# One layer of sparse attention and a gated recurrence: splits of the recurrence at a slot's head, a group of products half a step later, key roots by quarters

## Chip, core and metric

The kernel runs on one core of a Trainium2 chip. A core has a matrix engine (PE, whose weight loads the profile lists as PEld), a vector engine (DVE), a scalar engine (ACT), a general engine (POOL) and a queue engine for transfers (SP). Each works through its own list of instructions in order, and waits at an instruction until what it depends on has been signalled. The metric is the device time of one execution in microseconds; lower is better.

## What is computed

One inference step of a hybrid decoder layer, for a prompt of 512 tokens and for 8 sample sequences of 8 tokens each, 576 columns in all, in fp32. The reference, cut to what matters here:

```python
def _project(x, norm_g, w_in, q_norm_g, k_norm_g):
    z = jnp.einsum('btd,dc->btc', _rms(x, norm_g), w_in)
    ...                                        # q, kv, gates, x_rnn, g_rnn, ... are columns of z
    kv_sel = jnp.stack([_rms(kv[:, :, 1, 0], k_norm_g[1]), kv[:, :, 1, 1]], axis=2)
    kv_win = jnp.stack([_rms(kv[:, :, 2, 0], k_norm_g[2]), kv[:, :, 2, 1]], axis=2)

def _sel_win_sample(q, kv_sel_new, kv_win_new, sel_idx, sel_valid, cache_sel, page_table, cache_win, q_pos):
    ...                                        # softmax over cached and new keys, compressed branch beside it

def _rglru(x_ext, h0, conv_w, conv_b, w_rg, b_rg, w_ig, b_ig, lru_lambda):
    xc = conv_b
    for k in range(CONV_W):
        xc = xc + x_ext[:, k:k + T] * conv_w[k]
    xb = xf.reshape(B, T, RNN_BLOCKS, RNN_BLOCK_DIM)
    r = jax.nn.sigmoid(jnp.einsum('btnd,nde->btne', xb, w_rg).reshape(B, T, D_RNN) + b_rg)
    i = jax.nn.sigmoid(jnp.einsum('btnd,nde->btne', xb, w_ig).reshape(B, T, D_RNN) + b_ig)
    log_a = -LRU_C * r * jax.nn.softplus(-lru_lambda)
    a, u = jnp.exp(log_a), jnp.sqrt(-jnp.expm1(2.0 * log_a)) * (i * xf)
    ...                                        # h = a * h + u over the tokens
```

The two branches are gated, projected to 2048 columns, merged, and go through one output projection.

## The kernel before

**Products in slots.** Every large product is made of three products of halves: an operand is split into a rounded high part and the rest, and high by high, low by high and high by low are summed in one bank of PSUM (lines 1798 to 1800). The columns go in two halves of 288. A slot is 24 such matmuls: one output tile, one half of the columns, 8 blocks of the sum. The weights are split two slots or so ahead of their use: ACT makes `whi` (line 233), DVE makes `wlo` (line 239).

**What sets the order.** Nothing is scheduled by a planner while the chip runs. The program is written out slot by slot, and each engine gets its instructions in the order of writing. In one slot come, one after the other: the weights' high part; what `at(slot, f)` has put at the slot's head (`later`); the step of the prompt's or the samples' attention that is due; the weights' low part; the evacuation of a finished tile (`evac`: for a gate of the recurrence, an ACT line 576 and a DVE line 577); what `at(slot, f, True)` has put behind (`behind`); and last the slot's 24 matmuls. So for ACT and DVE, `later` stands ahead of the attention's step and the evacuation, `behind` after them.

**Keys of the prompt.** For each of four groups of heads, `norms` works the keys' root mean squares into the keys: `small` (lines 622 to 634), `root` (a reciprocal on line 639 and a product on line 640), `split` (lines 646 to 653). These stand in slots among the prompt's attention: scores on PE, row maxima on DVE (line 742), exponentials on ACT (line 746), the sums' reciprocal on DVE (lines 750 and 751), the scaling of the probabilities on POOL (line 754), and their transposition on PE (line 761).

**Samples.** `sample_steps` lists the samples' attention by `put(step, half, order, f)`: four pairs of sequences, a step is two slots, `half` says which of them, and `order` sorts within the slot; orders of one slot go from small to large. `x_turn_` (lines 1000 and 1004, PE) turns the probabilities and values of the compressed branch, `x_turned` (lines 1011 to 1013, ACT) copies them to `vx`, `x_out` (line 1021, 48 small matmuls on PE) multiplies them. `x_sum` (line 969) is a small sum that stands later. `s_turned` (line 1083, ACT) copies the turned probabilities of cached keys out of the banks `t`.

**Recurrence.** Eight chunks of 128 channels, `rnn_chunk(c, xr)`, called about every 12th slot beside the samples' attention. Its parts stand in the slots behind the call: the convolution's taps (lines 1276 and 1277, DVE), `split` (line 1221 on ACT and 1222 on DVE for the block weights `bd`, lines 1291 on ACT and 1292 on DVE for the channels `xb`), the gates' matmuls (line 1302, PE, into a bank `s` and a bank `t`) with their tanh (line 1305, ACT), `decay` (lines 1308 to 1310, ACT) and `scan` (lines 1315 to 1323). PSUM has two banks `g`, `s` and `t` each, and one `o` and one `m`; a bank's next use waits until its last reader has signalled.

The order in time is: projection of the prompt's heads with the prompt's attention (to about 720 us), the samples' attention with the recurrence (720 to 1024 us), the remaining projections and the output products (1025 to 1644 us).

Of the kernel before, what the change touches and what calls it, by code (L numbers as in the profile page):

```python
# [32 lines left out]
HF = 288  # L33
# [80 lines left out]
def nsa_rglru_step(ctx, tc, a, o):  # L114
# [15 lines left out]
    def bank(tag):  # L130
        t = ps.tile([128, 512], F, tag=tag, name=tag, bufs=banks[tag])
        current[tag] = (current[tag] + [t])[-banks[tag]:]
        return t
# [15 lines left out]
    def C(name):  # L149
        at, n = CST[name]  # L150
        return cst[:, at:at + n]

    def P(name, i=0):
        return par[:, PAR[name][0] + i:PAR[name][0] + i + 1]
# [36 lines left out]
    for n, (kind, m, units) in enumerate(tiles):  # L191
# [19 lines left out]
        for u in range(len(units)):  # L211
            late = len(units) == 1 or u == 0 and tiles[n - 1][0][0] == "G"
            at = base - 2 if late else base - 3 if u == 0 else base - 1
# [109 lines left out]
    for c in range(8):  # L323
        for b in range(2):
            k = 2 * c + b
            x = xs[c][:, b]
# [41 lines left out]
    def at(slot, fn, last=False):  # L368

        (behind if last else later).setdefault(slot, []).append(fn)  # L370

    now = [0]
# [13 lines left out]
    def store(fn, delay=2):  # L386
        at(now[0] + delay, fn)
# [3 lines left out]
    def evac(kind, h, b):  # L391
# [165 lines left out]
        elif name == "rx":  # L557
# [9 lines left out]
            if h == 1:  # L567
                A.activation(xr[:, 515:603].rearrange("p (b s) -> p b s", s=11)[:, :, 3:11],
                             b[:, n0:HF].rearrange("p (t b) -> p b t", b=8), AF.Copy)
                rnn_chunk(c, xr)  # L570
# [33 lines left out]
    def norms(g):  # L604

        k, v, rq = held["k"], held["ksq"], held["rq"]
        cc, sq = held["cc"]
        m = bank("m")
        T.matmul(m[:, :16], C("bones"), sq, start=True, stop=True)
        V.tensor_scalar(sq, m[:, :16], 1.0 / HD, EPS, op0=OP.mult, op1=OP.add)  # L610
        A.activation(sq, sq, AF.Sqrt)
        A.activation(rq, rq, AF.Sqrt)
        A.activation(v, v, AF.Sqrt)
        m = bank("t")
        T.transpose(m[:16, :128], cc, ident)
        vc = VCB[g % 2]
        A.activation(vc[:16, 0, :], m[:16, 64:128], AF.Copy)
        V.tensor_sub(vc[:16, 1, :], m[:16, 64:128], vc[:16, 0, :].bitcast(F))
        VC[g] = vc

        def small():
            V.reciprocal(sq, sq)
            V.reciprocal(rq, rq)
            RQ[g] = rq
            kc2 = pp["p"].tile([128, 32], R, tag="kc2", name="kc2", bufs=2)
            kc = pp["p"].tile([128, 16], F, tag="kc", name="kc", bufs=2)
            lo = slice(0, 64)
            V.scalar_tensor_tensor(kc[lo], cc[lo], P("gk0")[lo], sq[lo], OP.mult, OP.mult)
            for hl in range(2):
                d = slice(hl * 64, hl * 64 + 64)  # L630
                A.activation(kc2[d, 0:16], kc[lo], AF.Copy)
            for hl in range(2):
                d = slice(hl * 64, hl * 64 + 64)
                V.tensor_sub(kc2[d, 16:32], kc[lo], kc2[lo, 0:16].bitcast(F))
            KC[g] = kc2

        def root(h):
            hs = slice(h * HF, h * HF + HF)
            V.reciprocal(v[:, hs], v[:, hs])
            V.scalar_tensor_tensor(k[:, hs], k[:, hs], P("gk12"), v[:, hs], OP.mult, OP.mult)  # L640
            if h == 1:
                store(lambda: S.dma_start(o["kv"][2 * KG + g], k))

        def split(br):
            me = slice(br * 64, br * 64 + 64)
            V.tensor_copy(kn[(g % 2) * 64:(g % 2) * 64 + 64, g // 2, br, :], k[me, 512:576])
            kh = pp["a"].tile([128, SEQ], R, tag="k", name="kh", bufs=4)
            kl = pp["a"].tile([128, SEQ], R, tag="k", name="kl", bufs=4)
            other = slice(64 - br * 64, 128 - br * 64)
            A.activation(kh[me], k[me, :SEQ], AF.Copy)  # L650
            A.activation(kh[other], k[me, :SEQ], AF.Copy)
            V.tensor_sub(kl[me], k[me, :SEQ], kh[me].bitcast(F))
            V.tensor_sub(kl[other], k[me, :SEQ], kh[me].bitcast(F))
            K[g, br] = (kh, kl)

        for n, f in enumerate((small, lambda: root(0), lambda: root(1), lambda: split(0), lambda: split(1), lambda: ready.add(g))):
            if n in FULL:
                full.add(now[0] + 1 + n)
            at(now[0] + 1 + n, f, n < 5)

    ready, full = set(), set()
# [13 lines left out]
    for g in range(KG):  # L675
        for i in range(4):
            for br in range(3):
                x = Group()
# [473 lines left out]
    def sample_steps():  # L1152

        steps = {}

        def put(t, half, order, f, *args):
            steps.setdefault(2 * t + half, []).append((order, len(steps.get(2 * t + half, [])), f, args))

        for x in pairs:
            s = 2 + 6 * x.n
            if x.b[0].b >= KEPT:
                for y in x.b:
                    put(s - 5, 1, 0, c_fetch, y)
            put(s - 2, 0, 9, q_pair, x)
            e = s - 3 if x.n else s - 2
            put(e, 0, 0, c_square, x)
            put(e, 1, 5, c_norm, x)
            put(e, 1, 7, c_root, x)  # L1170
            put(e + 1, 1, 7, c_keys, x)
            put(s, 0, 4, x_scores, x)
            put(s, 0, 8, x_exp, x)
            put(s, 1, 7, x_prob, x)
            put(s, 1, 9, x_new, x)
            put(s + 1, 1, 5, x_sum, x)
            put(s + 1, 1, 6, x_select, x)
            for k, n2 in enumerate((4, 0, 1, 2, 3)):
                t = s + 1 + k
                put(t - 1, 0, 0, k_load, x, n2)  # L1180
                put(t, 1, 0, v_load, x, n2)
                put(t, 0, 4, k_scores, x, n2)
                put(t, 0, 8, k_max, x, n2)
                put(t, 0, 9, s_exp, x, n2)
                put(t + 1, 0, 1, s_turn, x, n2)
                put(t + 1, 0, 1.5, s_turned, x, n2)
                put(t + 2, 0, 2, s_out, x, n2)
            put(s + 5, 1, 9, s_factors, x)
            put(s + 6, 1, 7, s_total, x)
            put(s + 6, 1, 1, x_turn_, x)  # L1190
            put(s + 6, 1, 1.5, x_turned, x)
            put(s + 7, 0, 4.5, x_out, x)
            put(s + 7, 1, 8, s_sum, x)
            put(s + 8, 1, 5, s_fin, x)
            put(s + 8, 1, 8, s_put, x)
        for t in range(max(steps) + 1):
            fs = [f for _, _, f, _ in steps.get(t, [])]
            taken.extend(f for f in fs if f in (x_scores, k_scores, s_turn, x_turn_, c_norm))
            for _, _, f, args in sorted(steps.get(t, []), key=lambda e: e[:2]):
                f(*args)  # L1200
            yield (t + 1) / (max(steps) + 1)
# [15 lines left out]
    def split_bd(c):  # L1217
        t = bd[c]
        hi = rp_["p"].tile([128, 2, 128], R, tag="bdh", name="bdh", bufs=1)
        lo = rp_["p"].tile([128, 2, 128], R, tag="bdl", name="bdl", bufs=1)  # L1220
        A.activation(hi, t, AF.Copy)
        V.tensor_sub(lo, t, hi.bitcast(F))
        bd[c] = (hi, lo)
# [34 lines left out]
    def rnn_chunk(c, xr):  # L1258
# [26 lines left out]
        def split():  # L1285

            split_bd(c)
            for w in range(2):
                me, other = slice(w * 64, w * 64 + 64), slice(64 - w * 64, 128 - w * 64)
                t = p.tile([128, NT], R, tag=f"xb{w}", name="xb", bufs=1)  # L1290
                A.activation(t[me], xc[me], AF.Copy)
                V.tensor_sub(t[other], xc[me], t[me].bitcast(F))
                xb.append(t)
# [31 lines left out]
            if ("s", c) in held:  # L1325
                rnn_gated(c)

        at(now[0] + 2, split, True)

        def gate_0():  # L1330
            gate(0)
# [321 lines left out]
    for s, (n, h, u) in enumerate(slots):  # L1653
# [129 lines left out]
        for step, (h2, k) in enumerate([(h, k) for k in range(8)]):  # L1783
# [5 lines left out]
            hs = slice(h2 * HF, h2 * HF + HF)  # L1789
# [111 lines left out]
```

## Time and profile before

| | us |
|---|---|
| median of 3 runs | 1647.01 |
| lowest and highest | 1646.27 and 1648.58 |
| the profiled execution | 1646.57 |
| its span, first to last instruction | 1644.5 |
| PE busy | 1603.1 (97%) |
| DVE busy | 1104.0 (67%) |
| ACT busy | 775.9 (47%) |
| POOL busy | 305.7 (19%) |
[...]

A busy share says how much of the span an engine worked. PE's share leaves some 40 us in which it stood idle; the view of waits names for each of these pieces the bank or tile waited for, the line of the waiting instruction, and the instruction that ended the wait. A timeline shows the instructions of one engine in order of time with the idle time before each, and a view of windows gives the busy time of all engines and the granted clock in a stretch that one chooses.

### The profile page before, as it was taken

The numbers are of one execution on the slowest core, as the hardware profiler recorded it, in microseconds if no ns is written. First come the engines' busy times: TensorE is split into PE (matmuls) and PEld (weight loads), VectorE is DVE, ScalarE is ACT, GpSimd is POOL, SyncE is SP. The second block draws the span as 40 slices with busy tenths as digits, with TensorE's granted clock in tenths as the row PEclk, the third lists the DMA queues.
The fourth block names the chain that finished last, engine by engine and source line by source line (L and its number), as shares of the span: only waits on it lengthen the run. The fifth ranks groups of instructions, "written<-read, shape, count | busy, mean of one in ns | idle before, by whom it ended". The sixth has DMA issues, their size and how long they took to land.

```text
span 1644.5 us, 34197 instructions
## 1 busy us (share of the span) xinstructions
PE 1603.1 (97%) x13293; PEld 1550.9 (94%) x13293; DVE 1104.0 (67%) x2159; ACT 775.9 (47%) x1429; POOL 305.7 (19%) x361
## 2 busy tenths in 40 slices
PE   9999999999999999999898999999999999999999
PEld 8989989998999999998788889999999999999999
DVE  7768778766876786666566575766666433458785
ACT  6353545454445554448666677444444222234332
POOL 0014443533443345400000000000000111110000
PEclk9999999999999999999999999999999999999999
DMA  6178534433443344448575674633328444466431
GB/s 231 63 273 273 187 106 130 161 114 107 157 140 112 116 147 157 146 140 256 180 227 192 218 236 142 202 140 126 126 107 300 157 163 147 143 219 218 150 136 70
DMA packets 131956, 271.91 MB, mean 165 GB/s; under 512 B 19793, under 2 KB 59858, under 8 KB 131538
## 3 DMA queue, kind: packets, MB, share of 16 engines
q1 hardware_dynamic: 131794, 269.73, 49.0%
q8 instruction: 104, 1.70, 0.4%
q14 instruction: 58, 0.48, 0.1%
HBM read 235.04 MB, written 43.02 MB: 169 GB/s over the span
## 4 chain that ended last, share of the span: by engine, by line
PE 47%; ACT 3%; DVE 3%; issue 0%; DMA 0%; POOL 0%; SPq 0%; ACTq 0%
PE g L1798 9%; PE g L1799 9%; PE g L1800 9%; PE g L1448 2%; PE g L1447 2%; PE g L1446 2%; PE g L1548 2%; PE g L1547 2%; PE g L1546 2%; PE t L1448 1%; PE t L1446 1%; PE t L1447 1%; PE s L941 1%; PE s L1548 1%; PE s L1546 1%; PE s L1547 1%
## 5 line engine op out<-in xcount | busy, mean ns | idle before, releaser
L1798 PE MATMUL g<-xh,whi 128*128 128x288 f32 x1920 | 580.8, 303 | 0.1
L1800 PE MATMUL g<-xh,wlo 128*128 128x288 f32 x1920 | 569.8, 297 | 3.7 <-DVE wlo L239 3.7
L1799 PE MATMUL g<-xl,whi 128*128 128x288 f32 x1920 | 570.1, 297 | 0.1
L1798 PEld LDWEIGHTS g<-xh,whi 128*128 128x128 f32 x1920 | 364.8, 190 | 17.0 <-issue 14.4
L1800 PEld LDWEIGHTS g<-xh,wlo 128*128 128x128 f32 x1920 | 364.2, 190 | 4.2 <-DVE wlo L239 4.2
L1799 PEld LDWEIGHTS g<-xl,whi 128*128 128x128 f32 x1920 | 364.7, 190 | 1.7 <-DVE xl L321 0.3
L239 DVE TENSOR_TENSOR wlo<-raw,whi 128x1024 fp32r<-128x1024 f32 x164 | 215.7, 1315 | 73.8 <-ACT whi L233 73.2
L879 POOL TENSOR_TENSOR cr<-cr,wcs 128x512 f32<-128x512 f32 x128 | 182.3, 1430 | 144.5 <-DMA cr<-in_cmp 140.4
L233 ACT ACTIVATE whi<-raw 128x1024 fp32r<-128x1024 f32 x164 | 172.5, 1052 | 30.4 <-PE g L1799 16.5
L746 ACT ACTIVATE p<-p,sm,rq 128x128 f32<-128x128 f32 (+3 forms) x128 | 82.9, 648 | 143.1 <-DVE sm L743 143.0
L765 DVE TENSOR_TENSOR pt<-t,pt 128x512 fp32r<-128x512 f32 x96 | 66.1, 689 | 69.9 <-ACT pt L764 68.8
L754 POOL TENSOR_SCALAR p<-p,sm 128x128 f32<-128x128 f32 (+3 forms) x128 | 69.5, 555 | 226.7 <-DVE sm L751 125.5
L589 POOL TENSOR_TENSOR ur<-ur,tgi 128x288 f32<-128x288 f32 x32 | 25.7, 805 | 400.6 <-DVE tgi L588 304.8
L764 ACT ACTIVATE pt<-t 128x512 fp32r<-128x512 f32 x96 | 56.6, 593 | 73.6 <-PE t L761 73.0
L885 DVE TENSOR_REDUCE skvx<-cr 128x16 f32<-128x512 f32 x128 | 86.7, 678 | 2.6 <-POOL cr L879 1.7
L595 ACT ACTIVATE mh<-ur 128x288 fp32r<-128x288 f32 x32 | 14.2, 444 | 143.6 <-POOL ur L589 143.6
L1800 PE MATMUL g<-hrh,wlo 128*128 128x288 f32 x256 | 75.6, 295 | 0.0
L1800 PE MATMUL g<-oah,wlo 128*128 128x288 f32 x256 | 75.6, 295 | 0.0
L1799 PE MATMUL g<-hrl,whi 128*128 128x288 f32 x256 | 75.5, 295 | 0.0
L1798 PE MATMUL g<-hrh,whi 128*128 128x288 f32 x256 | 75.5, 295 | 0.0
L1799 PE MATMUL g<-oal,whi 128*128 128x288 f32 x256 | 75.5, 295 | 0.0
L1798 PE MATMUL g<-oah,whi 128*128 128x288 f32 x256 | 75.4, 295 | 0.0
(440 smaller groups left out, 3599.4 us busy)
## 6 DMA issues: line engine op xcount, KB each, us to landing
raw<-in_w_in SPq DMA_DIRECT2D x124, 512.0 KB, 3.7
cr<-in_cmp SPq DMA_DIRECT2D x128, 256.0 KB, 3.6
kr<-in_selk SPq DMA_DIRECT2D x128, 128.0 KB, 3.3
vr<-in_selv SPq DMA_DIRECT2D x128, 128.0 KB, 2.9
a<-in_w_in SPq DMA_DIRECT2D x28, 512.0 KB, 4.2
tgi<-tg SPq DMA_DIRECT2D x32, 288.0 KB, 4.2
yr<-in_w_out SPq DMA_DIRECT2D x18, 512.0 KB, 5.1
raw<-in_w_rnn SPq DMA_DIRECT2D x16, 512.0 KB, 4.7
```

The lines of the kernel that those rows point to most:

```text
L233: A.activation(hi, raw[k], AF.Copy)
L239: V.tensor_sub(lo, raw.pop(k), hi.bitcast(F))
L746: A.activation(p[:, :n], p[:, :n], AF.Exp, bias=sm[:, 1, r - r0:r - r0 + 1], scale=rq[:, i, r:r + 1], accum_out=sm[:, 2, r - r0:r - r0 + 1])
L754: G.tensor_scalar(p[:, :n], p[:, :n], sm[:, 3, r - r0:r - r0 + 1], 1.0, op0=OP.mult, op1=OP.mult)
L764: A.activation(hi, t, AF.Copy)
L765: V.tensor_sub(lo, t, hi.bitcast(F))
L879: G.tensor_tensor(v, v, wcs[:, :, None, :].to_broadcast([128, 4, 4, 32]), op=OP.mult)
L885: V.tensor_reduce(x.kvx[:, :, 8 + n * 4:12 + n * 4], v, axis=AX.X, op=OP.add)
L1446: T.matmul(gb[:, :HF], wh[:, i, :], r_h[:, HS[half]], start=begins and i == 0, stop=False, skip_group_check=True)
L1798: T.matmul(gb[:, :HF], wh[:, k, :], r_h[:, hs], start=kk == 0, stop=False)
L1799: T.matmul(gb[:, :HF], wh[:, k, :], r_l[:, hs], start=False, stop=False)
L1800: T.matmul(gb[:, :HF], wl[:, k, :], r_h[:, hs], start=False, stop=last and k == 7)
```

## The change

Three edits. First, the keys' `root` works on quarters of 144 columns in place of halves of 288: the first stands right behind `small` in the same slot, the others in the three slots after it, and the keys' two splits each one slot later than before. Second, `x_out` moves from half 0 (order 4.5) of its step to half 1 (order 1), one slot of 24 matmuls later. Third, the recurrence's `split` goes from `behind` to `later` of its slot; `decay` and `scan` stay behind.

```diff
--- before.py
+++ after.py
@@ -635,10 +635,10 @@
             KC[g] = kc2
 
         def root(h):
-            hs = slice(h * HF, h * HF + HF)
+            hs = slice(h * (HF // 2), (h + 1) * (HF // 2))
             V.reciprocal(v[:, hs], v[:, hs])
             V.scalar_tensor_tensor(k[:, hs], k[:, hs], P("gk12"), v[:, hs], OP.mult, OP.mult)
-            if h == 1:
+            if h == 3:
                 store(lambda: S.dma_start(o["kv"][2 * KG + g], k))
 
         def split(br):
@@ -653,7 +653,8 @@
             V.tensor_sub(kl[other], k[me, :SEQ], kh[me].bitcast(F))
             K[g, br] = (kh, kl)
 
-        for n, f in enumerate((small, lambda: root(0), lambda: root(1), lambda: split(0), lambda: split(1), lambda: ready.add(g))):
+        for n, f in enumerate((lambda: (small(), root(0)), lambda: root(1), lambda: root(2), lambda: root(3), lambda: split(0),
+                               lambda: (split(1), ready.add(g)))):
             if n in FULL:
                 full.add(now[0] + 1 + n)
             at(now[0] + 1 + n, f, n < 5)
@@ -1189,7 +1190,7 @@
             put(s + 6, 1, 7, s_total, x)
             put(s + 6, 1, 1, x_turn_, x)
             put(s + 6, 1, 1.5, x_turned, x)
-            put(s + 7, 0, 4.5, x_out, x)
+            put(s + 7, 1, 1, x_out, x)
             put(s + 7, 1, 8, s_sum, x)
             put(s + 8, 1, 5, s_fin, x)
             put(s + 8, 1, 8, s_put, x)
@@ -1325,7 +1326,7 @@
             if ("s", c) in held:
                 rnn_gated(c)
 
-        at(now[0] + 2, split, True)
+        at(now[0] + 2, split)
 
         def gate_0():
             gate(0)
```

What this does to the lists of the engines, at three places. The numbers of the lines from 656 on are one higher in the changed kernel.

DVE in the second group of keys, before, from the last row maximum of a head's scores to the factor of line 751:

```order
L742 ISA sm 128x1
L743 SCALAR_TENSOR_TENSOR sm<-sm,rq 128x2
L239 TENSOR_TENSOR wlo<-raw,whi 128x1024
L639 RECIPROCAL ksq<-ksq 128x288
L640 SCALAR_TENSOR_TENSOR kt<-kt,par,ksq 128x288
L885 TENSOR_REDUCE skvx<-cr 128x4x4
L750 RECIPROCAL sm<-sm 128x2
L751 TENSOR_TENSOR sm<-sm,gT 128x2
```

and now, to the same factor, line 752:

```order
L743 ISA sm 128x1
L744 SCALAR_TENSOR_TENSOR sm<-sm,rq 128x2
L239 TENSOR_TENSOR wlo<-raw,whi 128x1024
L639 RECIPROCAL ksq<-ksq 128x144
L640 SCALAR_TENSOR_TENSOR kt<-kt,par,ksq 128x144
L886 TENSOR_REDUCE skvx<-cr 128x4x4
L751 RECIPROCAL sm<-sm 128x2
L752 TENSOR_TENSOR sm<-sm,gT 128x2
```

A quarter stands where a half stood. The half that stood some ten rows further up (not shown) has become a quarter as well.

DVE around the split of chunk 1, before; line 926 reads the bank `t` of a norm (`c_root`), line 577 evacuates a gate tile:

```order
L1276 SCALAR_TENSOR_TENSOR xc<-xr,par,xc 128x512
L1277 SCALAR_TENSOR_TENSOR xc<-xr,par,xc 128x64
L926 TENSOR_SCALAR ssq<-t 128x256
L577 SCALAR_TENSOR_TENSOR rg<-rg,g 128x288
L1222 TENSOR_TENSOR bdl<-bd,bdh 128x256
L1292 TENSOR_TENSOR xb<-xc,xb 64x576 x2
L239 TENSOR_TENSOR wlo<-raw,whi 128x1024
```

and now:

```order
L1277 SCALAR_TENSOR_TENSOR xc<-xr,par,xc 128x512
L1278 SCALAR_TENSOR_TENSOR xc<-xr,par,xc 128x64
L1223 TENSOR_TENSOR bdl<-bd,bdh 128x256
L1293 TENSOR_TENSOR xb<-xc,xb 64x576 x2
L927 TENSOR_SCALAR ssq<-t 128x256
L577 SCALAR_TENSOR_TENSOR rg<-rg,g 128x288
L239 TENSOR_TENSOR wlo<-raw,whi 128x1024
```

The recurrence's three splits (lines 1223 and 1293) have gone ahead of the norm's reader (line 927) and of the evacuation.

ACT around the split of chunk 5, before; line 1083 copies turned probabilities out of both banks `t`, line 957 is the exponential of the compressed branch:

```order
L1323 ACTIVATE hout<-hh 128x8
L1083 ACTIVATE spt<-t 128x512 x2
L957 ACTIVATE se,ssm<-s,ssm 128x64 x2
L576 ACTIVATE rg<-g 128x288
L1221 ACTIVATE bdh<-bd 128x256
L1291 ACTIVATE xb<-xc 64x576 x2
L233 ACTIVATE whi<-raw 128x1024
```

and now:

```order
L1324 ACTIVATE hout<-hh 128x8
L1222 ACTIVATE bdh<-bd 128x256
L1292 ACTIVATE xb<-xc 64x576 x2
L1084 ACTIVATE spt<-t 128x512 x2
L958 ACTIVATE se,ssm<-s,ssm 128x64 x2
L576 ACTIVATE rg<-g 128x288
L233 ACTIVATE whi<-raw 128x1024
```

The split's copies (lines 1222 and 1292) have gone ahead of the copies out of the banks `t` (line 1084), the exponentials (line 958) and the evacuation.

## Rows read from the trace of the kernel before

**Rows 1.** PE waits: bank, line <- releaser: us, times, longest:

```profile
PE s L1302 <- DVE xb L1292: 7.7, 3, 5.2
PE t L761 <- POOL p L754: 6.6, 8, 2.7
PE o L1021 <- ACT vx L1012: 4.7, 2, 2.9
```

**Rows 2.** Timeline of DVE: start, us, line, operation, [idle before <- releaser]:

```profile
264.67 1.94 DVE L639 RECIPROCAL ksq<-ksq 128x288 f32<-128x288 f32 x1
...
267.87 0.16 DVE L751 TENSOR_TENSOR sm<-sm,gT 128x2 f32<-128x2 f32 x1
```

**Rows 3.** Timeline of DVE and PE, chunk 0:

```profile
729.59 1.75 DVE L931 RECIPROCAL ssq<-ssq 128x256 f32<-128x256 f32 x1
732.75 0.37 PE L941 MATMUL s<-skvx,qb 64*32 64x80 f32 x16
```

**Rows 4.** Timeline of PE at the place of rows 2:

```profile
268.97 0.33 PE L761 MATMUL t<-cst,p 128*128 128x128 f32 x1 [1.16 <-POOL p L754]
```

**Rows 5.** Timeline of DVE and PE, third group of keys:

```profile
410.24 0.16 DVE L751 TENSOR_TENSOR sm<-sm,gT 128x2 f32<-128x2 f32 x1
412.18 0.33 PE L761 MATMUL t<-cst,p 128*128 128x128 f32 x1 [2.70 <-POOL p L754]
```

**Rows 6.** Timeline of PE, chunk 2:

```profile
806.69 0.97 PE L1021 MATMUL o<-vx 80*32 80x64 f32 x22 [2.91 <-ACT vx L1012]
...
815.01 0.37 PE L1302 MATMUL s<-xb,bdh 128*128 128x288 f32 x1 [2.05 <-DVE xb L1292]
...
828.61 1.09 PE L1078 MATMUL t<-cst,sp 128*128 128x128 f32 x8 [0.48 <-ACT ti L1305]
```

**Rows 7.** Timeline of PE, chunk 5:

```profile
939.97 0.42 PE L1000 MATMUL t<-cst,se 128*80 128x128 f32 x2 [1.40 <-ACT spt L1083]
...
947.92 0.74 PE L1021 MATMUL o<-vx 80*32 80x64 f32 x22 [1.79 <-ACT vx L1012]
```

**Rows 8.** Timeline of ACT, PE and DVE, chunk 4:

```profile
895.18 1.38 ACT L1291 ACTIVATE xb<-xc 64x576 fp32r<-64x576 f32 x2
896.78 0.58 PE L1302 MATMUL s<-xb,bdh 128*128 128x288 f32 x1 [5.18 <-DVE xb L1292]
897.43 0.76 DVE L1315 TENSOR_TENSOR ti<-ti,tr 128x576 f32<-128x576 f32 x1
```

**Rows 9.** Timeline of DVE, chunk 2:

```profile
810.03 0.28 DVE L1277 SCALAR_TENSOR_TENSOR xc<-xr,par,xc 128x64 f32<-128x64 f32 x1
...
811.31 0.74 DVE L1066 CUSTOM_DVE_ANT_0 sp<-s,cst,ssm 128x504 f32<-128x504 f32 x1
...
814.12 1.54 DVE L1292 TENSOR_TENSOR xb<-xc,xb 64x576 fp32r<-64x576 f32 x2
```

**Rows 10.** Timeline of DVE and PE, chunk 1:

```profile
766.92 0.41 DVE L926 TENSOR_SCALAR ssq<-t 128x256 f32<-128x256 f32 x1
775.11 0.37 PE L1302 MATMUL s<-xb,bdh 128*128 128x288 f32 x1 [1.10 <-DVE ssm L1060]
```

**Rows 11.** Timeline of ACT, chunk 5:

```profile
939.34 1.06 ACT L1083 ACTIVATE spt<-t 128x512 f32<-128x512 f32 x2
...
944.05 1.38 ACT L1291 ACTIVATE xb<-xc 64x576 fp32r<-64x576 f32 x2
```

**Rows 12.** Timeline of DVE, chunk 5:

```profile
941.86 0.28 DVE L1277 SCALAR_TENSOR_TENSOR xc<-xr,par,xc 128x64 f32<-128x64 f32 x1
```

**Rows 13.** Timeline of PE, a wait in the prompt's stage:

```profile
536.58 0.47 PE L778 MATMUL o<-pt,vc 128*128 128x512 f32 x1 [1.82 <-DVE ores L787]
```

**Rows 14.** Windows: length, PE, PEld, DVE, ACT, POOL busy (x), PEclk, DMA, GB/s:

```profile
413.00:419.00 6.00, 6.00 (x48) 6.00 (x48) 5.92 (x11) 5.08 (x8) 3.80 (x3) 1.00 0.34 113
537.00:543.00 6.00, 6.00 (x35) 5.77 (x34) 4.28 (x7) 4.13 (x8) 1.11 (x1) 0.72 0.40 140
897.00:903.00 6.00, 6.00 (x27) 6.00 (x28) 4.30 (x8) 3.05 (x7) 3.04 (x6) 0.53 0.00 0
```

## Prediction

> **What bounds the kernel now.** I read the busy times first: PE works 97% of its span, so time can only be won where PE stands idle, some 40 us, or where its clock is low. The second view is the waits of PE [rows 1]. The three rows are those at which the change is aimed: gate matmuls of the recurrence that wait for the split on DVE (7.7 us), transposes of the prompt that wait for POOL's scaling (6.6 us), and `x_out` that waits for `vx` (4.7 us). What the reader is to see in them is only how long PE waited for the last of its conditions. What comes next to last is not in them; for that I read third the timelines of ACT, DVE and PE around each of the eight chunks and four key groups, and replayed each place with the new order and the old durations. Last come windows with the granted clock, since a wait can cost twice: behind some of them PE runs slower for a while. The profiled execution took 1646.57, 0.44 under the median of 1647.01; the sum is made on it and then moved to the median.
>
> **Key roots by quarters.** A half costs DVE 1.94 + 0.52 = 2.46 us; 1.94 is a reciprocal of 288 columns [rows 2], and one of 256 takes 1.75 [rows 3]. That is 6 ns a column and some 0.15 per instruction. The trace has no reciprocal of 144. Its bounds are half the long one, 0.97, and the long one itself, 1.94; by the line it is 1.05, and I take that, since the two lengths measured lie on it. With 0.3 for the product (between 0.26 and 0.52) a quarter is 1.35, 1.1 less than a half. DVE gets about 16 x 1.35 − 8 x 2.46 = 2 us more work in all, spread over four stretches in which PE doesn't wait for it. The gain is where a head's factor (line 751) stands behind a root and POOL behind the factor. In the second group two halves stand ahead of it, so it comes from 267.87 to 265.6 [rows 2]; the transposes behind it waited 1.16 [rows 4] and once more 0.34, and both waits go: −1.5. In the third group one half stands ahead: the factor at 410.24 comes 1.1 earlier, and of the wait of 2.70 [rows 5] about 1.05 goes. In the first group PE has no wait, in the fourth POOL waits for the exponentials, not for the roots: 0. Nothing comes back from the clock there, which stayed up behind this wait (below). Sum −2.6; bounds 0 and −4.5, all four waits of these two places.
>
> The fixed part per instruction speaks against cutting. [...]
>
> **x_out half a step later.** It costs nothing itself: the same 48 matmuls, 24 large ones ahead of them. Those cover the copies to `vx`, at both places where it waits for them: 2.91 in chunk 2 [rows 6] and 1.79 in chunk 5 [rows 7]. Whether the 4.7 are won depends on what PE reaches next, so they are counted below.
>
> **The split at the head, chunk by chunk.** ACT's two copies take 1.38 and DVE's two subtractions 1.54 [rows 8, 9]. Both need the taps, the last work of the slot before. So the head of the slot now holds both engines until the taps are done, and everything that the slot had ahead of the split stands behind it.
>
> *Chunk 0:* the reciprocal of the compressed keys (line 931), at 729.59, now waits for ACT's copies and DVE's subtractions, until about 731.9. The keys are done 2.3 later, about 734.3 in place of 732.0; PE's scores read them at 732.75 without a wait [rows 3], and now wait 1.4. **+1.4**.
>
> *Chunk 1:* the norm's reader (line 926) at 766.92 [rows 10] moves behind the subtractions, to 769.5 or so. It holds a bank `t` that the transposes of line 1078 want at about 768: a new wait of some 1.9. Later PE's gate matmuls waited 1.10 for line 1060 [rows 10], which doesn't move; that takes up the difference but for **+0.7**.
>
> *Chunk 2:* `x_out` no longer waits (2.91), and the channels are ready earlier: taps end 810.31, subtractions 812.6 in place of 815.7 [rows 9]. But the row maxima (line 1066), done at 812.05 [rows 9], now stand behind the subtractions and end at 812.6 + 1.8 = 814.4. The gate matmuls' bank `s` waits for them, and so do ACT's exponentials, evacuation and weights: 2.35 later, less the 1.7 of the split's copies that are no longer in between. All that follows on ACT and DVE is 0.65 later, up to the tanh that frees the bank for line 1078 at 828.61 [rows 6], on which PE waited already. PE saves 5 us and waits for them there: **+0.7**.
>
> *Chunk 4:* the largest wait, 5.18 [rows 8]. The split now comes ahead of the evacuation with its table load, and the gate matmuls start at 895.1, not 896.78. The scan stands where it was (line 1315 at 897.43 [rows 8]), the next weights and the tanh wait for it, and PE meets them at about 903: **−0.5**. The clock stays low: a wait of 3.5 is left.
>
> *Chunk 5:* ACT's copies out of the banks `t` (line 1083) ran at 939.34; the split's copies now stand ahead of them, and these wait for the taps, until 942.14 [rows 11, 12]. So they end at 943.5, the first bank is free at 944.05, and PE's turn of line 1000 starts at 944.1 in place of 939.97 [rows 7]. Its wait of 1.40 becomes 5.5: +4.1. The 1.79 of `x_out` go: **+2.3** at the gate matmuls, behind which no wait is left to take it up. *The others:* chunk 3 +0.1, chunks 6 and 7 nothing; their waits are 0.5 or none.
>
> **The clock.** [...] So a wait of 5.5 in chunk 5 takes about 6 x (1 − 0.53) = **2.8** more. The bounds are 0 and 2.8; I take 2.8, since the nearest wait in length paid it. For chunk 1's 1.9 the bounds are 0 and 6 x (1 − 0.72) = 1.7; I take 0, as a longer wait, the 2.70, passed without it. In chunk 2 PE will stand some 4.5 us before its gate matmuls, and a low clock behind that costs nothing: at 0.53 the next 24 matmuls take some 5.4 us instead of 3.0, and PE still comes to line 1078 before the bank is free.
>
> Sum: −2.6 + 1.4 + 0.7 + 0.7 + 0.1 − 0.5 + 2.3 + 2.8 = **+4.9**. The profiled execution goes to 1651.5, the median to **1651.9**.
>
> **Rivals.** *All waits come back:* nothing that passed behind the split is waited for. Then 7.7 + 4.7 [rows 1] + 2.6 + 2.8 of clock behind the 5.18 go, 17.8 in all: 1629.2, faster. The size of the rows speaks for it; against it stand the readers of banks in chunks 0, 1, 2 and 5 that the split has passed. The point that decides is chunk 5: if line 1000 starts by 941 and chunk 2's line 1078 before 826, it is this. Chance 0.12. *The bank of chunk 5 is not the one wanted:* line 1000 keeps its start and the rest holds, 4.9 − 4.1 − 2.8 = −2.0, 1645.0, no measurable difference: 0.06. *The wait of chunk 5 comes without the low clock:* +2.1, 1649.1, no measurable difference: 0.22. *The clock falls in chunk 1 too:* +6.6, 1653.6, slower: 0.20. The forecast itself has 0.40.
>
> **How the numbers follow.** A measurement of this kernel can tell about 0.2%, 3.3 us, from no change: under 1643.7 is faster, over 1650.3 slower. So faster 0.12, the same 0.06 + 0.22 = 0.28, slower 0.60. The range leaves out the first rival and little else. Below it takes in 1645.0 with a microsecond for the roots' bound, 1644.0; above it takes in 1653.6 and the roots at nothing in part, 1655.5.
>
> **What would show it.** In the changed profile: row maxima and factors ahead of line 751 by 1 to 2 us at 265 and 409, and the transposes' waits there gone and at 1.6; new waits of PE at the scores of 732.8 and at line 1078 near 768; line 1000 in chunk 5 waiting about 5.5 us with a granted clock near 0.5 behind it; no wait before `x_out`, and in its place a wait of some 4.5 us before the gate matmuls of chunk 2, at about 813.5. I am wrong if line 1000 doesn't wait there, or if the gains of chunk 2 last beyond 829.

## The result, and the profile of the changed kernel

| | before | changed |
|---|---|---|
| median, us (8 runs each) | 1646.78 | 1656.62 |
| lowest and highest | 1645.58 and 1648.58 | 1652.11 and 1661.5 |
| the profiled execution | 1646.57 | 1655.24 |
| its span | 1644.5 | 1653.5 |

The ratio is 1.0059 with a 95% interval of 1.0042 to 1.0077: slower, by 9.7 us (6.9 to 12.7). The direction was forecast, the size was twice the 4.9 forecast, and 1656.6 lies above the range's upper end of 1655.5. In this section and the next, a lag is the time at which PE starts the same instruction in one profiled execution, less that in the kernel before.

PE is busier, not idler: its share is the same, and it has worked 5 us longer at the same matmuls, since more of them ran at the lower clock (mean granted clock 0.989 of full speed, 0.992 before). The page, part 1:

```profile
PE 1608.0 (97%) x13293; PEld 1555.3 (94%) x13293; DVE 1107.7 (67%) x2175; ACT 775.8 (47%) x1429; POOL 306.6 (19%) x361
```

The waits of PE in the changed kernel (bank and line, releaser: us, times, longest; lines from 656 on are one higher). They answer to [rows 1]:

```profile
PE t L1001 <- ACT spt L1084: 5.6, 1, 5.6
PE g L1801 <- DVE wlo L239: 5.3, 4, 2.7
PE t L762 <- POOL p L755: 4.7, 6, 1.8
PE s L1303 <- DVE ssm L1066: 4.7, 1, 4.7
...
PE s L1303 <- DVE xb L1293: 3.8, 2, 3.5
PE t L1079 <- DVE ssq L927: 3.4, 2, 1.9
...
PE s L942 <- DVE skvx L934: 1.5, 1, 1.5
```

The wait for `vx` has gone from the list, the waits for POOL have fallen from 6.6 to 4.7 us and those for `xb` from 7.7 to 3.8: each of the three edits did what it says. At the top stand waits that were not there or were small: the turn for line 1084 (5.6), weights (5.3 in place of 3.7), the gate matmuls for the row maxima (4.7), the norm's reader (3.4 in place of 1.5), the compressed keys (1.5). Where they stand, in the timeline of PE (idle before the instruction, and what ended it), for chunks 0, 1, 2, 4 and 5; they answer to [rows 3], [rows 10], [rows 6], [rows 8] and [rows 7]:

```profile
735.88 0.60 PE L942 MATMUL s<-skvx,qb 64*32 64x80 f32 x16 [1.47 <-DVE skvx L934]
...
772.93 0.63 PE L1079 MATMUL t<-cst,sp 128*128 128x128 f32 x4 [1.87 <-DVE ssq L927]
...
817.91 0.58 PE L1303 MATMUL s<-xb,bdh 128*128 128x288 f32 x1 [4.69 <-DVE ssm L1066]
...
900.23 0.58 PE L1303 MATMUL s<-xb,bdh 128*128 128x288 f32 x1 [3.46 <-DVE xb L1293]
...
948.80 0.65 PE L1001 MATMUL t<-cst,se 128*80 128x128 f32 x2 [5.63 <-ACT spt L1084]
```

Chunk by chunk the lag grew by 1.5 in chunk 0, 1.0 in chunk 1, 0.8 in chunk 2 and 0.15 in chunk 3, fell by 0.5 in chunk 4, and grew by 4.3 in chunk 5; in all 7.3 from 732 us on, where 7.5 were forecast. ACT around chunk 5 shows how, against [rows 11]:

```profile
943.92 0.40 ACT L1222 ACTIVATE bdh<-bd 128x256 fp32r<-128x256 f32 x1
946.74 1.39 ACT L1292 ACTIVATE xb<-xc 64x576 fp32r<-64x576 f32 x2 [2.42 <-DVE xc L1278]
948.15 1.08 ACT L1084 ACTIVATE spt<-t 128x512 f32<-128x512 f32 x2
```

The block weights' copy is done at once. Then ACT stands 2.42 us for the taps (line 1278), with the copies out of the banks `t` behind it in its queue, and PE's turn waits for the first of these. In chunk 2 the row maxima (line 1067) now follow the subtractions on DVE and end at 818.6; the gate matmuls took the first of their two banks at 817.91. The timeline of DVE, against [rows 9]:

```profile
815.23 1.54 DVE L1293 TENSOR_TENSOR xb<-xc,xb 64x576 fp32r<-64x576 f32 x2 [0.41 <-ACT xb L1292]
...
817.89 0.74 DVE L1067 CUSTOM_DVE_ANT_0 sp<-s,cst,ssm 128x504 f32<-128x504 f32 x1
```

So the recurrence went as forecast. The other 1.6 us of lag stood there before it, at 732, where the forecast had a gain of 2.6. The timeline of PE in the prompt's stage:

```profile
142.97 0.40 PE L1801 MATMUL g<-xh,wlo 128*128 128x288 f32 x1 [1.29 <-DVE wlo L239]
...
410.64 0.33 PE L762 MATMUL t<-cst,p 128*128 128x128 f32 x1 [1.84 <-POOL p L755]
...
603.15 0.38 PE L739 MATMUL s<-kh,q 128*128 128x256 f32 x1 [0.44 <-DVE sm L743]
...
612.29 0.78 PE L762 MATMUL t<-cst,p 128*128 128x128 f32 x2 [0.80 <-POOL p L755]
```

Both waits near 269 are gone, and the 2.70 at 412 became 1.84, as forecast ([rows 4, 5]). But there is a wait of 1.29 for the weights' low part at 142.97, which is in no row of before, and two small ones near 603 and 612 (before, none and 0.5). DVE's timeline shows what stands ahead of those weights:

```profile
133.55 1.68 DVE L653 TENSOR_TENSOR kl<-kt,kh 64x512 fp32r<-64x512 f32 x1
...
136.88 1.68 DVE L653 TENSOR_TENSOR kl<-kt,kh 64x512 fp32r<-64x512 f32 x1
...
138.59 0.62 DVE L701 TENSOR_TENSOR ce<-s,cst 128x64 f32<-128x64 f32 x4
...
141.70 1.22 DVE L239 TENSOR_TENSOR wlo<-raw,whi 128x1024 fp32r<-128x1024 f32 x1
```

The second subtraction of each key split (line 653) took 1.68 us, and the weights (line 239) begin at 141.70. The same rows in the timeline of DVE of the kernel before:

```profile
132.76 0.68 DVE L653 TENSOR_TENSOR kl<-kt,kh 64x512 fp32r<-64x512 f32 x1
...
135.84 0.69 DVE L653 TENSOR_TENSOR kl<-kt,kh 64x512 fp32r<-64x512 f32 x1
...
139.59 1.22 DVE L239 TENSOR_TENSOR wlo<-raw,whi 128x1024 fp32r<-128x1024 f32 x1
```

In both kernels both splits stand ahead of these weights, and from 131 us on DVE works up to them without a pause that the timeline marks. In the kernel before the weights were done at 140.81, about a microsecond before PE used them at 141.77; in the changed kernel they were done at 142.92, with PE ready at 141.68. DVE's instructions between took longer: the two subtractions by 1.0 each, and line 706 (705 before) took 1.10 in place of 0.42. The second of the long subtractions began while POOL's product was running, as the timeline of POOL of the changed kernel shows:

```profile
136.65 1.36 POOL L880 TENSOR_TENSOR cr<-cr,wcs 128x512 f32<-128x512 f32 x1 [1.97 <-DMA cr<-in_cmp]
```

The windows behind the wait of 1.84 and behind chunk 5's wait (length, busy us of PE, PEld, DVE, ACT and POOL with their instructions, granted clock, DMA share, GB/s) answer to [rows 14]:

```profile
412.00:415.00 3.00, 3.00 (x17) 3.00 (x16) 2.46 (x6) 1.72 (x3) 1.80 (x3) 0.62 0.53 163
949.00:955.00 6.00, 6.00 (x34) 5.72 (x36) 4.08 (x21) 4.07 (x13) 0.00 (x0) 0.62 0.16 37
```

The clock was 0.62 behind 1.84 us of waiting, where it had been 1.00 behind 2.70 in the kernel before. That cost 1.3 us of the roots' gain in this execution. Step by step, the lag went from −0.2 at 140 us to +1.3 behind the wait for the weights, to −0.7 behind 269, to −1.5 at 410.64, to −0.2 behind the low clock there, and with +0.5, +0.8 and +0.3 near 578, 602 and 611 to the +1.6 at 732.

### The profile page after: what moved, and what is told of

Read it like the earlier page. It is cut to its first block, busy times and chain, and to the rows that moved or that the text cites. A ratio compares the mean times of both kernels' runs of the same rounds, so it can differ in the third digit from the quotient of the medians.

```text
span 1653.5 us, 34210 instructions
## 1 busy us (share of the span) xinstructions
PE 1608.0 (97%) x13293; PEld 1555.3 (94%) x13293; DVE 1107.7 (67%) x2175; ACT 775.8 (47%) x1429; POOL 306.6 (19%) x361
## 4 chain that ended last, share of the span: by engine, by line
PE 47%; ACT 3%; DVE 3%; issue 0%; DMA 0%; SPq 0%; ACTq 0%
PE g L1799 9%; PE g L1800 9%; PE g L1801 9%; PE g L1448 2%; PE g L1447 2%; PE g L1449 2%; PE g L1549 2%; PE g L1548 2%; PE g L1547 2%; PE s L942 1%; PE t L1447 1%; PE t L1448 1%; PE t L1449 1%; PE s L1549 1%; PE s L1547 1%; PE s L1548 1%
```

## The experiments

Where no other is named, a ratio is to the kernel before, run on the same chip, with its 95% interval; the medians of before were 1646.3 to 1647.2. One permille is 1.65 us.

### The three edits alone

```diff
 e1: only the root by quarters and its list of slots, as in the change
 e2
-        at(now[0] + 2, split, True)
+        at(now[0] + 2, split)
 e3
-            put(s + 7, 0, 4.5, x_out, x)
+            put(s + 7, 1, 1, x_out, x)
```

> Of the three edits only the keys' roots by quarters, with the keys' splits a slot later. Theory A (the quarters win at two places of the prompt's stage, but the splits that stand a slot later put DVE's work in front of the next weights): PE's waits for POOL at 269 gone and at 412 about a microsecond shorter, a new wait for the weights' low part near 143 of 1.3 us, and PE some 1.5 us late after the fourth group; in sum 0 to 2 us slower than before, 1647 to 1649. Theory B (what I forecast: only the two gains): 2.6 us faster, 1644.2.

Measured: 1649.73 us, 1.0013 (1.0003 to 1.0024), 2.2 us slower. The timeline of PE in its profiled execution has the new wait for the weights, and the wait for POOL at 2.45:

```profile
141.96 0.40 PE L1801 MATMUL g<-xh,wlo 128*128 128x288 f32 x1 [0.48 <-DVE wlo L239]
...
408.75 0.33 PE L762 MATMUL t<-cst,p 128*128 128x128 f32 x1 [2.45 <-POOL p L755]
```

The profiled execution itself was a quick one (span 1643.9; its lag at 731 us is −2.0). Its windows show part of why: the clock stayed up behind the wait of 1.82 at 388 and fell behind the one at 408, just the other way round than in the kernel before, and it stayed up behind the wait of 1.82 at 535 as well, where the kernel before had 0.72.

```profile
389.00:395.00 6.00, 6.00 (x49) 5.87 (x48) 4.40 (x7) 4.55 (x9) 3.12 (x2) 1.00 0.45 148
409.00:415.00 6.00, 5.66 (x33) 5.59 (x32) 4.06 (x8) 1.85 (x4) 4.19 (x4) 0.72 0.45 144
535.00:541.00 6.00, 6.00 (x47) 5.73 (x46) 4.43 (x7) 4.53 (x9) 1.26 (x2) 1.00 0.41 138
```

The kernel before at the first of these places, against [rows 14] for the other two:

```profile
390.00:396.00 6.00, 6.00 (x34) 5.87 (x35) 4.94 (x8) 3.94 (x8) 3.73 (x3) 0.72 0.45 150
```

> Only the recurrence's splits at the head of their slot. Theory A (the cost is in what the split has passed: readers of banks in chunks 0, 1, 2 and above all 5): 7 us slower, 1652 to 1656, with a wait of 5.5 us before the turn in chunk 5 and a granted clock of about 0.5 behind it, although the edit of the compressed values' products is not in. Rival C (the loss comes from the products that stand half a step later): within 2 us of before.

Measured: 1655.89 us, 1.0053 (1.0039 to 1.0067), 8.7 us slower. The wait of chunk 5 is there without the other edits:

```profile
947.63 0.65 PE L1000 MATMUL t<-cst,se 128*80 128x128 f32 x2 [5.66 <-ACT spt L1083]
```

> Only the compressed values' products a slot later. Theory A (chunk 2 hangs on the split, chunk 5 on nothing behind): the wait of 1.8 in chunk 5 goes and is won, the 2.9 in chunk 2 turn up again before the gate matmuls, so 1.8 us faster, 1645.0. Rival C: 2 us slower or more. Rival D (each wait of the table comes back): 4.7 us faster and more with the clock, 1640 to 1642.

Measured: 1647.43 us, 0.9998 (0.9989 to 1.0007): no change, which none of the three theories had. The timeline of PE in chunk 2:

```profile
817.42 0.58 PE L1302 MATMUL s<-xb,bdh 128*128 128x288 f32 x1 [5.96 <-DVE xb L1292]
```

and the six us from there:

```profile
817.00:823.00 6.00, 5.58 (x25) 5.61 (x26) 5.30 (x21) 3.24 (x6) 0.00 (x0) 0.56 0.99 313
```

The 2.91 and the 2.05 of [rows 6] have become one wait of 5.96 before the gate matmuls, with the clock at 0.56 behind it. In the kernel before, the low clock (0.50 from 807.25 to 810.25) came behind the first of the two, and the second wait covered it. In this execution, the slowest of its eleven (1651.28), chunk 2 lost 1.4 us and chunk 5 won 1.3.

### What turned the roots' gain into a loss

```diff
 e4: halves, splits a slot later
-        (small, lambda: root(0), lambda: root(1), lambda: split(0), lambda: split(1), lambda: ready.add(g))
+        (small, lambda: root(0), lambda: root(1), lambda: None, lambda: split(0), lambda: (split(1), ready.add(g)))
 e5: quarters, splits where they were
+        (lambda: (small(), root(0)), lambda: root(1), lambda: (root(2), root(3)), lambda: split(0), lambda: split(1), lambda: ready.add(g))
```

> The roots in halves as before, but the keys' splits a slot later. Theory A (it is the later splits that cost, not the quarters): the new wait for the weights near 143 and the delay after the fourth group without the gains, 2 to 4 us slower, 1649 to 1651. Theory B (the place of the splits costs nothing): no change, 1646.8.

Measured: 1648.62 us, 1.0006 (0.9996 to 1.0016). The sign is not settled by this run. Its profiled execution has waits for the weights of 0.5 at 141.6 and 0.3 at 579.6, and 0.5 at 604.

> Only the keys' roots by quarters, but with the splits in the slots in which they stood before: the third and fourth quarter share a slot. If the later splits are what turns the roots' gain into a loss: no wait for the weights' low part near 142, the waits at 269 shorter, 1 to 2.6 us faster than before, 1644 to 1646. If cutting into quarters costs by itself (more instructions on DVE): as with the later splits, 2 us slower, 1649.

Measured: 1646.54 us, 0.9996 (0.9987 to 1.0005): 0.65 us faster by the median, no measurable difference. No wait for weights stands near 142 or 579. Half of the wait near 269 is left, since two quarters now share a slot there:

```profile
268.39 0.33 PE L761 MATMUL t<-cst,p 128*128 128x128 f32 x1 [0.40 <-POOL p L754]
...
410.72 0.33 PE L761 MATMUL t<-cst,p 128*128 128x128 f32 x1 [1.84 <-POOL p L754]
```

> The whole change, but with the keys' splits in their old slots (third and fourth quarter in one slot). If the later splits turn the roots' gain into a loss here as they did alone: no wait for the weights' low part near 143 and none of 0.4 near 603, 2 to 3.5 us faster than the changed kernel, 1653 to 1654.5. If it doesn't matter beside the loss in the recurrence: as the changed kernel, 1656.6.

Measured: 1653.16 us, 1.0048 (1.0036 to 1.0061), 3.5 us under the changed kernel's median and 1.8 by the ratios, whose intervals overlap. In all three pairs the later splits were the slower side (1.0013 to 0.9996, 1.0006 to 1, 1.0059 to 1.0048). In the five profiled executions with later splits, the wait for weights near 142 was 0.5, 0.5, 1.3, 2.7 and 3.6 us; in the nine without, it was missing in six and 1.0, 1.1 and 1.4 in three. So the wait goes with the later splits, but not with them alone, and not through their place in DVE's queue, since both stand ahead of these weights in every one of the kernels. What the eight executions with the wait have in common is that between 131 us and the weights' end at least one instruction of DVE that reads two tensors began while POOL's product ran, and took 0.8 to 1.1 us longer. Rows of e1, e4 and e7 (the last with the splits in their old slots), in this order:

```profile
139.58 2.32 DVE L239 TENSOR_TENSOR wlo<-raw,whi 128x1024 fp32r<-128x1024 f32 x1
...
138.65 1.28 DVE L705 TENSOR_TENSOR ce<-ce,csm 128x256 f32<-128x256 f32 x1
...
139.58 1.40 DVE L706 TENSOR_TENSOR ce<-ce,rq 128x256 f32<-128x256 f32 x1
```

The kernel before, where lines 705 and 706 took 0.42 each and the weights 1.22:

```profile
138.78 0.42 DVE L705 TENSOR_TENSOR ce<-ce,csm 128x256 f32<-128x256 f32 x1
139.24 0.42 DVE L706 TENSOR_TENSOR ce<-ce,rq 128x256 f32<-128x256 f32 x1
```

Of the six executions without the wait, two (e2, e11) had one such long instruction there and four had none. In the longest wait, the 3.58 of e12, DVE had also stood idle for 0.92 us just before 131, at the weights ahead of these, for their high part from ACT.

### Where the split costs

```diff
 e6: the changed kernel with
+        at(now[0] + 2, split, c == 5)
 e7: the kernel before with a third list, run between the samples' step and the evacuation
+        for f in mid.pop(s, []):
+            f()
         for e in evs:
             evac(*e)
...
+        mid.setdefault(now[0] + 2, []).append(split)
```

> The whole change, except that chunk 5 keeps its split behind. If the delayed copies out of the banks t in chunk 5 cost 4.1 us and the low clock behind that wait 2.8, less the 1.8 of the products' wait, that is 5 us faster than the changed kernel, 1651 to 1652. If the loss of the change is spread over the chunks alike (each split that has passed something costs about a microsecond), 1 to 2 us faster than it, 1655.

Measured: 1650.77 us, 1.0023 (1.0013 to 1.0033), 5.9 us under the changed kernel. The turn of chunk 5 waits as it did before:

```profile
947.66 0.42 PE L1001 MATMUL t<-cst,se 128*80 128x128 f32 x2 [1.40 <-ACT spt L1084]
```

and the clock behind it stays up:

```profile
948.00:954.00 6.00, 6.00 (x111) 4.80 (x110) 4.87 (x14) 3.61 (x10) 0.48 (x3) 1.00 0.34 132
```

> The kernel before with the recurrence's split ahead of the evacuation, but behind the samples' step of its slot: it passes the gate tile's two instructions and no reader of a bank s or t. If the loss comes from the readers of banks that the split at the head passes: no new waits in chunks 0, 1, 2 and 5, the wait of 5.2 in chunk 4 about 3.5, 0.5 to 2 us faster than before, 1645 to 1646.3. If any move of the split ahead costs: 2 us slower or more.

Measured: 1645.44 us, 0.9989 (0.998 to 0.9998), 1.8 us faster. None of the waits of chunks 0, 1 and 5 appears, and chunk 4's wait of 5.18 is 3.45:

```profile
896.44 0.37 PE L1302 MATMUL s<-xb,bdh 128*128 128x288 f32 x1 [3.45 <-DVE xb L1292]
```

> As the last, with the compressed values' products a slot later too. If the products' later place wins its 1.8 in chunk 5 and only moves the wait of chunk 2 to the gate matmuls: 1 to 3 us faster than before, 1644 to 1646. If the longer wait in chunk 2 brings a low clock where it is not absorbed, as the run with that edit alone showed: no faster than the last, 1646 to 1648.

Measured: 1647.06 us, 1.0003 (0.9993 to 1.0013): no measurable difference, 1.6 us over the run before by the median, with intervals that touch. Its trace has the exchange of e3: chunk 2 lost 1.7 us and chunk 5 won 1.2. So the products' later place for all pairs appears to give back what the split won.

> The whole change but for the products of the compressed values, which stand where they stood. If their later place is worth nothing once the split stands at the head (the turn's wait of 5.6 us in chunk 5 covers the 1.8 that they waited): within 2 us of the changed kernel, 1655 to 1658.5. If their later place was part of the loss: 3 us or more faster, 1653 or less. If it hid a loss: slower than 1659.

Measured: 1655.54 us, 1.0056 (1.0043 to 1.0069), within the changed kernel's interval. `x_out` at its old place does not wait in chunk 5; the turn's wait covers it:

```profile
949.33 0.65 PE L1001 MATMUL t<-cst,se 128*80 128x128 f32 x2 [5.65 <-ACT spt L1084]
...
957.46 0.54 PE L1022 MATMUL o<-vx 80*32 80x64 f32 x24
```

### A version that beats both

```diff
 e9: the kernel before with
+            put(s + 7, *((1, 1) if x.n == 2 else (0, 4.5)), x_out, x)
 e10: e9, the quarters of e5 and the split of e7
```

> The compressed values' products a slot later for the third pair of sequences alone, the one of chunk 5; the other pairs as before. If the edit wins in chunk 5 and gives it away in chunk 2 (a longer wait before the gate matmuls, with a low clock behind it): 1.3 to 1.8 us faster than before, 1645.0 to 1645.5, better than the same edit for all pairs, which was within 0.9 of before. If the wait of 1.8 in chunk 5 costs nothing that comes back: no change, 1646.8.

Measured: 1644.73 us, 0.999 (0.9981 to 0.9999), 1.7 us faster. Of the waits of `x_out` one is left (view of PE's waits):

```profile
PE o L1021 <- ACT vx L1012: 2.9, 1, 2.9
```

and chunk 2's gate matmuls wait less than 1 us (timeline of PE; behind the 2.91 the clock was low, and in the slot ahead of them matmuls of 288 columns started 0.24 us apart from 807.44 to 811.76 and 0.13 to 0.14 apart behind that):

```profile
813.64 0.37 PE L1302 MATMUL s<-xb,bdh 128*128 128x288 f32 x1 [0.73 <-DVE xb L1292]
```

> Together: the roots by quarters with the splits in their old slots, the recurrence's split ahead of the evacuation but behind the samples' step, and the products a slot later for the third pair alone. If the parts add (0.65, 1.75 and 1.5 us): 3 to 4 us faster than before, 1643 to 1644. If the parts' gains are taken up by the low clock, which comes behind a wait of about 2 us or not: 1 to 2 us faster, 1645 to 1646.

Measured: 1644.43 us, 0.9984 (0.9975 to 0.9993), 2.6 us faster than the kernel before and about 12 faster than the changed one. That lies between the two cases expected; the runs don't separate it from e9.

## Why the prediction was wrong in size

**What held.** Each wait that the replay of the split foresaw came, at its place and nearly at its length: 1.47 us at the scores of chunk 0 (1.4 forecast), 1.87 at the transposes of chunk 1 (1.9), 4.69 before the gate matmuls of chunk 2 (4.5), 3.46 in chunk 4 (3.5), 5.63 in chunk 5 (5.5). The lag over this stretch came to 7.3 against 7.5. (Two of the small sums are a tenth or so off by their own figures: 734.3 less 732.75 is 1.55 and not 1.4, and 1.9 less 1.10 is 0.8 and not 0.7.) The split alone measured 8.7 (6.4 to 11), and with chunk 5 put back 5.9 of the change's 9.8 went, where 2.3 + 2.8 were counted. The first rival, that the table's waits come back, is out: the point that was to decide it, line 1000 of chunk 5 by 941, was missed by 8 us. So are the rival in which that turn keeps its start and the one in which its wait comes without the low clock. The low clock in chunk 1, the last rival, came behind the same wait of 1.9 in three of the five executions with it, and not in the one of the changed kernel.

**What failed: the term of the roots.** It stood at −2.6 with bounds of 0 and −4.5; measured alone it is +2.2 (0.5 to 4.0). The difference of 4.8 is as large as the whole miss. Taken the other way, as the change less the split alone (9.7 less 8.7), roots and products together come to +1.0, and each of these figures is uncertain by 2 to 3 us. By either the gain of 2.6 is missing. Two steps of its working were wrong.

The first is the work of DVE in the first and the fourth group of keys, entered at 0. The prediction gave DVE 2 us more work "spread over four stretches in which PE doesn't wait for it", and asked which waits quarters could shorten; it did not ask how much time DVE had to spare in these stretches. The quarters were sized well; a reciprocal of 144 columns took 1.04 us where 1.05 was taken:

```profile
L639 DVE RECIPROCAL ksq<-ksq x16: 1036/1044/1053, 121.3 to 559.1; 128x144 f32<-128x144 f32 x16
```

Both gains came in the changed kernel's trace, 1.9 us near 269 and 0.9 at 411. But near 142 DVE had only about a microsecond to spare, and a lag of 1.6 came there; another 1.6 came behind the fourth group, near 578, 602 and 611. What used up the spare time near 142 is seen: instructions that took longer beside POOL's product. Why they met it more often is not. A split's subtraction near 135 met it in four of the five executions with later splits and in one of the nine without, and with the splits in their old slots the loss was gone by the median (e5), and in the whole change 3.5 us of it by the medians (e11), 1.8 by the ratios. The intervals of each pair touch or overlap, so the runs point to the later splits three times over without settling their price. How much is due to them, and how much to the quarters' own additional work, stays open: no run kept POOL's products away from these instructions.

The second is the low clock, read from one execution. The windows of [rows 14] stand behind the waits of 2.70, 1.82 and 5.18 us, in this order. That the clock stayed at 1.00 behind the first was taken to mean that this wait never costs anything beyond its length, and that shortening it brings all that is cut off. In the 14 profiled executions of this study the same wait (1.8 to 2.7 us) had the low clock behind it in 9, the one of 1.8 near 390 in 8, the one of 1.8 near 537 in 9. The prediction had 1.7 for such a case as an upper bound in chunk 1 alone and nowhere else. In the changed kernel's trace it took 1.3 of the gain. It is not the whole loss: the mean granted clock is on record for every run, 0.9927 over the 12 of e1 and 0.9931 over the 29 of the kernel before, and by that it took about 0.7 of the 2.3 us by which e1's mean span is longer. Over the eight runs of the changed kernel, which spread over 9 us, span and mean clock go together only in part (correlation −0.54). Where e1's runs lost the rest is not shown, since its one trace is of a quick execution.

One trace does not settle a term of this size either. Up to 731 us the programs of e2, e3, e7, e8 and e9 are that of the kernel before, and their lags at 731 us go from −1.3 to +2.4.

**A term that was mis-sized.** The low clock of chunk 5 was entered at 2.8 us behind the wait, by the 0.53 of [rows 14] behind the 5.18 of chunk 4. The trace has 0.62 over the six us behind it and a lag that grew by 2.1 there; a part of the low stretch lay inside the wait (granted clock 0.50 from 947 on, and PE started at 948.80), where it costs nothing.

**What the sum should have been.** By the runs: 2.2 (or about 1, inside the change) for the roots, 7.3 to 8.7 for the split, nothing for the products. That is 8 to 11, and the measured 9.7 lies in it.

## To carry to other kernels

When a step is moved to the head of an engine's slot, ask not what waits for it but what it waits for, and which bank's readers are queued behind it: the split waited for taps, and everything in its slot waited with it. Moving it ahead of the evacuation alone, behind the bank's readers, took the part of the gain that was there. When an edit gives an engine more work or moves its steps, ask how much time it has to spare before the next instruction that another engine needs, and not only whether that engine waits today: DVE had about a microsecond near 142 us. And a wait of a length behind which the clock fell in some executions and not in others (1.8 to 2.9 us here) should enter a sum with a chance, not with what one trace showed.

## What the runs showed of the hardware

The same wait had the low clock behind it in some executions and not in others; what decides it is not shown. Over the 14 profiled executions, no wait of PE between 1.3 and 1.6 us had it behind it, those of 1.8 to 2.9 sometimes had, and every one of 3.4 us or more had. Behind the same wait of 2.74 us at 98 it fell in twelve and stayed up in two; the changed kernel and e10, in the same six us:

```profile
98.00:104.00 6.00, 6.00 (x27) 6.00 (x27) 3.94 (x8) 1.80 (x4) 0.00 (x0) 0.53 1.08 398
```

```profile
98.00:104.00 6.00, 4.40 (x31) 4.16 (x32) 4.16 (x8) 1.62 (x4) 0.00 (x0) 1.00 1.09 414
```

Where it fell, the stretch at the lower level (0.50 of full speed from 897 to 902 us in the kernel before) mostly took about 1.7 or about 3.4 us of PE's time, summed from one less the granted clock. And near 135 us a subtraction of 64 partitions by 512 columns on DVE took 0.67 to 0.69 us, but 1.67 to 1.78 when it began while POOL's product was running; this met one or two of them in five of the 14 executions. In the changed kernel the second long one ended 0.55 us after POOL's product (138.56 and 138.01), a little less than the 0.69 that such a subtraction took alone; why it took longer is not shown.
